# Another order of all steps in a two-layer diffusion backbone

## The chip, the cores and the metric

The kernel runs on one core of one Trainium2 chip. The metric is the device time of one execution in microseconds (us); lower is better. The engines named below are TensorE (PE, matmuls), VectorE (DVE), ScalarE (ACT), GpSimd (POOL) and SyncE (SP), whose queue issues most transfers (DMAs).

## What is computed

The reference is a backbone of two layers over 512 latent tokens and 256 context tokens of width 1024. Layer 0 mixes the tokens by windowed grouped-query attention with a sink per head, layer 1 by a gated MLP over chunks of 128 tokens. Each mixer is followed by a SwiGLU feed-forward network (FFN) with 2816 hidden channels. Before and after each part stands an RMS norm with shift, scale and gate from a modulation vector ("Ada" in the kernel). Cut to what matters here:

```python
def rmsnorm(x, g):
    xf = x.astype(jnp.float32)
    y = xf * lax.rsqrt(jnp.mean(xf * xf, axis=-1, keepdims=True) + RMS_EPS)
    return (y * g.astype(jnp.float32)).astype(x.dtype)

def modulate(h, shift, scale):
    return h * (1 + scale) + shift

def chunk_gmlp(h, w_in, b_in, ln_g, ln_b, w_s, b_s, w_o):
    bsz, n, _ = h.shape
    z = jax.nn.gelu(h @ w_in + b_in, approximate=False)
    u, v = jnp.split(z, 2, axis=-1)
    v = layernorm(v, ln_g, ln_b).reshape(bsz, n // CHUNK, CHUNK, B_GROUPS, B_GROUP_W)
    mixed = jnp.einsum('gpq,bnqgc->bnpgc', w_s, v) + b_s.T[None, None, :, :, None]
    return (u * mixed.reshape(bsz, n, B_WIDTH)) @ w_o

def swiglu(h, w_in, w_out):
    gate, up = jnp.split(h @ w_in, 2, axis=-1)
    return (jax.nn.silu(gate) * up) @ w_out
```

## The kernel before

Matrix products are done in parts: each float32 operand is split into a rounded high part (`high`, a cast on ACT, L412) and a low part (`low`, a subtraction on DVE, L419), and a product is three matmuls, high by high, low by high and high by low. Weights come from HBM as units of 128 x 2048 (1 MB, `w_raw`, two buffers) by `Stream.fetch` on SP's queue (L489); the split parts `w_hi` and `w_lo` have four buffers each.

The FFN's first half (class `FFN`, L1466) works through hidden units of 128 channels for gate and up. From unit 0 of layer 1, and over most of layer 0, it uses seven products per unit in place of eight (`product`, L1626, its matmuls at L1635), on sums of weight quarters (`diff`, L1587, on DVE, on POOL for the first units) and sums of the tokens. The results of a unit's products are gathered by `keep` (ACT, L1642), `up2`, `up1`, `gate1` (DVE, L1646 to L1654), `silu` (ACT) and `gates` (DVE). In the names, `f0product_21_6` is layer 0, unit 21, product 6.

The second half multiplies by `w_out`. Two unit pairs at its ends are plain products (`plain7`, matmuls at L1846); between them stands `seven` (L1853): the seven products of a Strassen scheme over a 2 x 2 division, each in four parts p, `product7(i, p)` (L1819). Quarters 11, 21, 22 and 12 of the weights come in halves by `fetch7` (L1746, SP). Quarter 12 is loaded twice. One copy goes into two buffers of its own, from which DVE makes the sums of 12 and 11 (`t7`, L1801). The other goes into the buffer `t7` (eight blocks of 1024 columns; quarter 21 has the second four), where POOL adds quarters 22, 11 and 21 to it in place by transfers that accumulate (`t7_add`, L1807, 256 KB each). Half 0 of quarter 22 uses the `w_raw` buffer that half 1 of quarter 12 had, and `t7_3` is the last to read that. `w7_high` and `w7_low` split a block, `a7_high` and `a7_low` the tokens; `save7` (ACT) and `add7` (DVE) hold partial results.

The end of a part is a `Chain` per block t of 128 tokens: `square_y` (ACT, L439), `rstd_y` (DVE L448 and POOL L449), `gain_y` (DVE, L1319), `add_x` (DVE, L1323), `store` (SP). Block 3 of the last layer is done in two halves of 512 columns.

At the start `warm` (L686) keeps PE at work on zeros, `turn_in` (L692) transposes the input, `rope_turn` (L909) the table of the rotary embedding, and `ada0_rows` (L709) makes the first modulation rows from weights `ada`, which load in pieces `ada0_fetch`.

The order of all this is a table. The program is written as steps; `at(time, step, ...)` gives a step a name (`key`) and its rank in the list `ORDER` (L41), and `run_plan()` issues the steps sorted by rank:

```python
        plan.append((rank.get(key, len(rank) + time), len(plan), key, step, args))

    def run_plan():
        for _, _, key, step, args in sorted(plan, key=lambda e: e[:2]):
            step(*args)
```

The order of the list is kept on each engine, and each engine and each issuing queue works in that order. A step that waits holds up all later steps of its engine; a load on SP that waits for its buffer holds up all later loads. Which buffer of a ring a step gets follows from the order as well.

Of the kernel before, what the change touches and what calls it, by code (L numbers as in the profile page):

```python
# [46 lines left out]
ada0_fetch_1 dma#2 ada0_fetch_2 ada0_fetch_4 square_in_2 turn_in_0_0 ada0_rows_out_0 turn_in_0_1 rstd_in_2 norm_in_2_0
norm_in_2_1 ada0_cols_0 turn_in_2_0 whigh_0_0 ada0_rows_1 rope_turned_0 turn_in_2_1 turned_in_0_0 ada0_rows_out_1
turn_in_3_0 <lambda> ada0_done_0 modulate0_ctx_0 ada0_cols_1 wlow_0_0 modulated_ctx_0 kv_0_4 kv_0_5 turned_in_2_0
ada0_done_1 turned_in_3_0 modulate0_0 modulated_high_0 modulated_low_0 wfetch_0_1 modulated_high_1 ada0_rows_2  # L50
ada0_rows_out_2 kv_0_2 turned_in_2_1 modulate0_ctx_1 modulate0_1 modulated_ctx_1 ada0_cols_2 kv_0_1 whigh_0_1 kv_0_0
modulated_low_1 kv_1_4 kv_1_1 kv_1_2 kv_1_5 ada0_done_2 ada0_fetch_3 rope_turned_1 modulate0_ctx_2 turned_in_0_1
modulate0_2 m2start wlow_0_1 modulated_high_2 ada0_rows_4 modulated_ctx_2 ada0_rows_3 ada0_rows_out_4 ada0_cols_4
ada0_done_4 kv_1_0 ada0_rows_out_3 ada0_cols_3 wfetch_1 whigh_1_0 wlow_1_0 whigh_1_1 kv_2_4 modulated_low_2 kv_0_3
ada0_fetch_5 kv_1_3 kv_2_3 kv_2_1 ada0_done_3 modulate0_3 modulated_high_3 modulate0_ctx_3 ada0_rows_5 modulated_ctx_3
kv_3_4 kv_2_5 kv_3_5 modulate0_ctx_4 modulated_ctx_4 modulated_high_4 kv_2_2 kv_4_5 kv_2_0 modulated_low_3
ada0_rows_out_5 ada0_cols_5 kv_3_2 kv_3_3 m2fetch_0 m2add_0 kv_3_0 kv_3_1 dma#3 ada0_fetch_6 ada0_rows_6 m2add_1
modulate0_4 <lambda>#2 ada0_done_5 modulated_high_5 modulate0_ctx_5 ada0_fetch_7 ada0_rows_7 modulated_low_4 kv_4_2
wfetch_2 kv_4_3 ada0_rows_out_6 ada0_cols_6 wlow_1_1 modulate0_5 modulated_low_5 whigh_2_0 wlow_2_0 ada0_done_6
modulate0_6 kv_4_4 ada0_rows_out_7 kv_4_0 m2fetch_1 m2add_2 m2add_3 modulated_high_6 modulated_low_6 kv_5_0 q_first_0_0  # L60
kv_5_3 whigh_2_1 ada0_cols_7 dma#4 modulated_ctx_5 ada0_done_7 modulated_high_7 wlow_2_1 modulate0_ctx_6 kv_4_1 kv_5_1
q_first_0_1 q_first_0_2 q_first_0_3 q_first_0_4 q_first_0_5 kv_5_2 kv_6_3 kv_5_5 modulate0_7 modulated_ctx_6 q_first_0_6
kv_6_0 kv_5_4 m2fetch_2 modulated_low_7 modulate0_ctx_7 kv_7_3 kv_6_1 m2add_4 kv_6_4 m2add_5 m2fetch_3 kv_6_2 kv_7_2
wfetch_3 kv_6_5 kv_7_0 q_first_0_7 kv_7_1 modulated_ctx_7 m2add_6 m2add_7 kv_7_5 kv_7_4 q_first_1_0 table_Exp k_copy_2_0
k_copy_2_1 q_rows_0 v_copy_0 k_copy_0_0 k_rope_2 k_add_2 k_copy_0_1 v_copy_1 k_copy_4_0 k_copy_4_1 v_copy_2 k_rope_0
v_copy_3 q_first_1_1 q_first_1_2 q_first_1_3 q_first_1_4 q_first_1_5 q_first_1_6 q_first_1_7 k_turn_2_1 k_add_0 v_copy_4
# [2167 lines left out]
```

## Time and profile before

| | us |
|---|---|
| median of 3 runs | 1097.65 (1097.63 to 1099.7) |
| the profiled execution | 1098.59 |
| its span | 1096.8 |
| PE busy | 1077.8 (98%), 6894 instructions |
| DVE busy | 939.1 (86%) |
| ACT busy | 601.0 (55%) |
| POOL busy | 263.1 (24%) |
| DMA traffic | 181.25 MB, mean 165 GB/s |

The parts of the span: start to 23 us, attention to 300, hidden units of layer 0 to 488, its second half to 570 or so, the gating layer to 780, hidden units of layer 1 to 970, the rest its second half. Busy time of an engine says little by itself; the windows below set the busy time of each engine in a stretch against the length of the stretch, and the timeline says of single instructions how long the engine had been idle and what ended that.

### The profile page before, as it was taken

How to read it: one execution, taken by the hardware profiler on the slowest of the kernel's cores; microseconds unless marked ns; L12 is line 12 of the kernel's file. 1: busy time of each engine (PE TensorE's matmuls, PEld its weight loads, DVE VectorE, ACT ScalarE, POOL GpSimd, SP SyncE). 2: the span in 40 equal slices, each digit the busy share in tenths (PEclk: the TensorE clock that was granted, in tenths of full speed). 3: DMA queues.
4: the chain of work that ended last, by engine and by line, in shares of the span. 5: the costliest groups of instructions: out<-in, count | busy, mean ns of one | idle time of the engine just before them, and what ended most of it. 6: DMA issues, size and time to landing. Idle time of an engine off the chain costs nothing.

```text
span 1096.8 us, 17794 instructions
## 1 busy us (share of the span) xinstructions
PE 1077.8 (98%) x6894; PEld 948.3 (86%) x6894; DVE 939.1 (86%) x1382; ACT 601.0 (55%) x1055; POOL 263.1 (24%) x268
## 2 busy tenths in 40 slices
...
GB/s 357 285 153 169 179 109 46 78 188 177 77 174 192 212 117 196 170 213 248 238 88 78 203 271 236 192 197 73 96 134 120 113 154 143 113 229 315 172 28 77
DMA packets 50392, 181.25 MB, mean 165 GB/s; under 512 B 5370, under 2 KB 9722, under 8 KB 39172
## 3 DMA queue, kind: packets, MB, share of 16 engines
...
q8 instruction: 54, 0.88, 0.3%
...
## 4 chain that ended last, share of the span: by engine, by line
PE 89%; DVE 5%; DMA 3%; issue 1%; ACT 1%; SPq 0%; DVEq 0%; POOLq 0%; POOL 0%; ACTq 0%
PE f L1635 36%; PE y L1819 12%; PE y L479 7%; PE y L1846 6%; PE v L479 4%; PE s_ps L1099 2%; PE pT_ps L1132 2%; PE o_ps L1148 2%; PE q_ps L861 1%; DMA t<-in_w 1%; PE fa L471 1%; PE fa L473 1%; PE fa L472 1%; PE u L2054 1%; PE u L2053 1%; PE u L2052 1%
## 5 line engine op out<-in xcount | busy, mean ns | idle before, releaser
L1635 PE MATMUL f<-H,w_hi 128*128 128x256 f32 x960 | 177.8, 284 | 0.5 <-DVE fc L1646 0.5
L1635 PEld LDWEIGHTS f<-H,w_hi 128*128 128x128 f32 x960 | 150.0, 192 | 1.3 <-DVE fc L1646 1.0
L1635 PE MATMUL f<-H,w_lo 128*128 128x256 f32 x480 | 135.8, 283 | 0.0
L1819 PE MATMUL y<-w_hi,s 128*128 128x512 f32 x448 | 120.6, 390 | 2.5 <-ACT s L412 1.3
L1635 PE MATMUL f<-S,w_hi 128*128 128x256 f32 x640 | 118.5, 284 | 0.5 <-ACT fc L1642 0.5
L412 ACT CAST w_hi<-T 128x1024 fp32r<-128x1024 f32 x80 | 83.7, 1047 | 58.7 <-PE f L1635 41.5
L412 ACT CAST w_hi<-w_raw 128x1024 fp32r<-128x1024 f32 x90 | 94.0, 1054 | 31.1 <-PE f L1635 11.3
L1819 PEld LDWEIGHTS y<-w_hi,s 128*128 128x128 f32 x448 | 83.9, 188 | 20.8 <-DVE s L419 1.8
L419 DVE TENSOR_TENSOR w_lo<-w_raw,w_hi 128x1024 fp32r<-128x1024 f32 (+1 forms) x81 | 96.1, 1192 | 6.4 <-ACT w_hi L412 6.1
L1635 PEld LDWEIGHTS f<-S,w_hi 128*128 128x128 f32 x640 | 99.8, 192 | 0.9 <-ACT fc L1642 0.7
L419 DVE TENSOR_TENSOR w_lo<-T,w_hi 128x1024 fp32r<-128x1024 f32 x80 | 97.3, 1219 | 2.6 <-ACT w_hi L412 2.6
L1635 PEld LDWEIGHTS f<-H,w_lo 128*128 128x128 f32 x480 | 92.1, 192 | 0.0
L1635 PE MATMUL f<-S,w_lo 128*128 128x256 f32 x320 | 90.6, 283 | 0.0
L1642 ACT COPY fc<-f 128x256 f32<-128x256 f32 x120 | 43.6, 372 | 84.2 <-PE f L1635 75.6
L1807 POOL DMA_DIRECT2D t<-in_w x48 | 42.5, 955 | 178.3 <-DMA t<-in_w 105.1
L581 DVE SCALAR_TENSOR_TENSOR acc<-ada_k,sc,acc 128x1024 f32<-128x1024 f32 x56 | 71.6, 1278 | 6.1 <-DMA ada_k<-in_ada 5.7
L595 POOL DMA_DIRECT2D acc<-acc x8 | 6.9, 868 | 286.2 <-DVE acc L581 279.1
L1819 PE MATMUL y<-w_lo,s 128*128 128x512 f32 x224 | 69.3, 391 | 1.1 <-DVE w_lo L419 1.1
L1126 POOL TENSOR_SCALAR p<-p,st 128x512 f32<-128x512 f32 (+1 forms) x64 | 59.8, 948 | 27.5 <-DVE st L1122 14.5
L1635 PE MATMUL f<-H,x 128*128 128x256 f32 x480 | 64.1, 283 | 0.0
L1110 ACT ACTIVATE p<-s_ps,st 128x512 f32<-128x512 f32 (+1 forms) x64 | 47.3, 741 | 25.9 <-DVE st L1105 22.3
L1635 PEld LDWEIGHTS f<-S,w_lo 128*128 128x128 f32 x320 | 61.4, 192 | 0.0
...
## 6 DMA issues: line engine op xcount, KB each, us to landing
w_raw<-in_w SPq DMA_DIRECT2D x67, 1024.0 KB, 5.4
ada_k<-in_ada SPq DMA_DIRECT2D x56, 512.0 KB, 5.9
ada_raw<-in_ada SPq DMA_DIRECT2D x12, 1024.0 KB, 5.4
w<-in_w SPq DMA_DIRECT2D x12, 1024.0 KB, 7.6
...
ada<-in_ada SPq DMA_DIRECT2D x8, 1024.0 KB, 8.4
t<-in_w SPq DMA_DIRECT2D x8, 1024.0 KB, 10.7
w_raw<-in_w SPq DMA_DIRECT2D x10, 512.0 KB, 7.3
```

What stands on the lines that cost most here:

```text
L412: nc.scalar.copy(out=hi, in_=src)
L419: (eng or nc.vector).tensor_tensor(out=v(lo), in0=v(src), in1=v(hi).bitcast(F32), op=ALU.subtract)
L479: nc.tensor.matmul(dst, l, w[:, n * 512:(n + 1) * 512], start=first and i == 0, stop=last and i == 2)
L581: nc.vector.scalar_tensor_tensor(out=self.acc, in0=self.raws.pop(k), scalar=sc[:, k:k + 1], in1=self.acc, op0=ALU.mult, op1=ALU.add)
L1099: nc.tensor.matmul(dst, q, keys, start=i == 0, stop=i == 1)
L1110: nc.scalar.activation(out=p[:, 0:self.n], in_=self.s[j], func=AF.Exp, scale=-1.0, bias=self.st[:, 4 + j:5 + j], accum_out=self.st[:, 8 + ...
L1126: nc.gpsimd.tensor_scalar(out=p, in0=p, scalar1=self.st[:, 12 + j:13 + j], scalar2=1.0, op0=ALU.mult, op1=ALU.mult)
L1635: nc.tensor.matmul(dst, l[:, w], r[:, k, :], start=first and k == 0 and j == 0, stop=k == 3 and j == 2, skip_group_check=True)
L1642: nc.scalar.copy(out=self.c[n][:, i * 256:(i + 1) * 256], in_=self.ps[n, 1 if i == 1 else 0])
L1807: nc.gpsimd.dma_start(out=self.tt[:, p * D + 512 * i:p * D + 512 * (i + 1)], in_=a["w"][F2[self.layer] + 1 + 2 * p + i][:, c:c + 512], acc ...
L1819: nc.tensor.matmul(self.bank7(i, j), st[:, c:c + P], w[:, z * 512:(z + 1) * 512], start=i == 1 and p == 0 and l == 0 and z == 0, stop=p == ...
L1846: nc.tensor.matmul(self.y[t][n], st[:, x + t * P:x + (t + 1) * P], parts[h][w][:, n * 512:(n + 1) * 512], start=v == 0 and h == 0 and i == ...
```

## The change

Only the table `ORDER` is another one. It has the same 3317 names, so each step and each instruction is there as often as before, and all buffers have the sizes and counts they had. A name stands 14.9 places from where it stood in the mean; the largest moves are 338 places up and 473 down. The file has two lines more, so that L1819 before is L1821 after. A few lines of the diff:

```diff
--- before.py
+++ after.py
@@ -39,359 +39,361 @@
 
 
 ORDER = """
...
-f0product_21_1 f0set_split_0 f0gate1_20 whigh_32_0 f0silu_18_1 f0fetch7_12_0_big f0keep_21_0 f0s7_S3_0 f0gates_18
-f0product_21_6 f0gates_19 f0silu_20_0 f0silu_20_1 m1halve_0 m1halve_512 m1total_0_slot wlow_32_0 whigh_32_1
-f0product_21_2 f0gate1_21 wlow_32_1 m1done_0 f0keep_21_2 f0product_21_7 f0keep_21_1 f0product_21_3 f0fetch7_11_0_raw
...
-f0product7_1_1 f0product7_1_2 f0a7_high_7_0 f0w7_high_7_1 f0a7_low_2_0 f0t7_3 f0w7_low_7_0 f0a7_low_7_0 f0s7_S2_0
...
-f0w7_high_7_3 f0a7_high_7_3 f0w7_high_7_2 f0w7_low_7_2 f0a7_high_7_2 f0w7_high_2_3 f0a7_low_7_2 f0s7_S2_2 f0a7_low_7_3
-f0w7_high_2_2 f0a7_high_2_2 f0w7_low_7_3 f0t7_add_0_11 f0s7_S2_3 f0t7_1 f0a7_low_2_2 f0product7_7_0 f0product7_7_1
...
+f0product_20_7 f0part_high_21_1 m1add_chunk_6 f0diff_21_4 f0part_high_21_3 f0product_21_1 f0up2_20 f0product_20_3
...
+whigh_32_0 f0gates_18 f0part_high_21_2 f0product_21_6 f0silu_20_0 f0part_low_21_2 f0keep_21_2 whigh_32_1 m1fetch_chunk_7
+m1fetch_gain wlow_32_0 f0silu_20_1 f0gates_19 wlow_32_1 f0product_21_5 f0keep_21_1 f0product_21_7 f0product_21_2
+f0up2_21 f0take7_0 f0product_21_4 m1add_chunk_7 m1halve_512 f0up1_20 f0gates_20 m0done_512 f0fetch7_12_0_big
...
+f0product7_1_1 f0t7_add_0_22 f0t7_0 f0w7_low_2_0 f0product7_1_2 f0a7_low_1_3 f0w7_high_7_0 f0s7_S3_2 f0t7_3
...
+f0product7_7_1 f0t7_add_0_11 f0w7_high_7_2 f0a7_high_2_2 f0w7_high_7_3 f0w7_low_7_2 f0s7_S2_1 f0w7_high_2_2 f0a7_low_7_2
+f0s7_S2_2 f0product7_7_2 f0a7_high_2_3 f0a7_low_2_2 f0w7_high_2_3 f0w7_low_7_3 f0product7_7_3 f0w7_low_2_2 f0a7_high_3_0
...
```

The pieces below show three places of it, in the order of issue on one engine.

ACT in `seven` of layer 0. `w7_5664`, `t7_5724` and the like are loaded quarters; an `s7` cast is of tokens, `act4_3425`, `act4_3971`, `act4_4430`, `act4_5055` being parts p = 0 to 3. Before:

```order
L412 CAST w_hi_5909<-t7_5724 128x1024
L412 CAST s7_5912<-act4_5055 128x512
L412 CAST w_hi_5914<-t7_5724 128x1024
L412 CAST s7_5918<-act4_4430 128x512
L412 CAST w_hi_5920<-t7_5724 128x1024
L412 CAST w_hi_5926<-t7_5724 128x1024
L412 CAST s7_5929<-act4_4430 128x512
L412 CAST s7_5986<-act4_3971 128x512
```

and in the change, where the parts are `act4_3494`, `act4_4037`, `act4_4447`, `act4_4976`:

```order
L414 CAST w_hi_5948<-t7_5694 128x1024
L414 CAST s7_5951<-act4_4447 128x512
L414 CAST w_hi_5953<-t7_5694 128x1024
L414 CAST w_hi_5958<-t7_5694 128x1024
L414 CAST s7_5975<-act4_4976 128x512
L414 CAST w_hi_5978<-t7_5694 128x1024
```

Before, `w_hi_5909` and `w_hi_5914` are blocks (7,3) and (7,2), then come `w_hi_5920`, block (2,3), and `w_hi_5926`, block (2,2). In the change `w_hi_5948` is (7,2), `w_hi_5953` is (7,3), and then comes `w_hi_5958`, block (2,2), ahead of `w_hi_5978`, block (2,3).

DVE in the hidden units of layer 1, from the last reader of unit 6's weights on. Unit 8's weights use the same buffer and load when it is free. Before, with unit 6 in `w_raw_8171` and unit 8 in `w_raw_8525`:

```order
L419 TENSOR_TENSOR w_lo_8441<-w_raw_8171,w_hi_8440 128x1024
L1650 TENSOR_TENSOR fc_8384<-f1_8371,fc_8384 128x256
L581 SCALAR_TENSOR_TENSOR acc_8443<-ada_k_7951,sc_69,acc_8443 128x1024
L1595 TENSOR_TENSOR T_8490<-w_raw_8401 128x512
L1646 TENSOR_TENSOR fc_8384<-f0_8324,fc_8384 128x256
L419 TENSOR_TENSOR w_lo_8473<-T_8366,w_hi_8472 128x1024
L1595 TENSOR_TENSOR T_8490<-w_raw_8401 128x512
L419 TENSOR_TENSOR x0_8510<-w_raw_8401,x0_8510 128x512
L1595 TENSOR_TENSOR T_8490<-T_8490,w_raw_8401 128x512
L1665 TENSOR_TENSOR act4_8362<-fc_8384,silu_8529 128x2x256
L1595 TENSOR_TENSOR T_8490<-w_raw_8401,T_8490 128x512
L419 TENSOR_TENSOR w_lo_8545<-T_8490,w_hi_8544 128x1024
```

and in the change, with unit 6 in `w_raw_7906` and unit 8 in `w_raw_8466`:

```order
L421 TENSOR_TENSOR w_lo_8449<-w_raw_7906,w_hi_8448 128x1024
L1667 TENSOR_TENSOR act4_8361<-fc_8110,silu_8484 128x2x256
L1648 TENSOR_TENSOR fc_8408<-f0_8329,fc_8408 128x256
L1597 TENSOR_TENSOR T_8534<-w_raw_7979 128x512 x2
L421 TENSOR_TENSOR x0_8503<-w_raw_7979,x0_8503 128x512
L1597 TENSOR_TENSOR T_8534<-T_8534,w_raw_7979 128x512
L583 SCALAR_TENSOR_TENSOR acc_7639<-ada_k_8464,sc_69,acc_7639 128x1024
L421 TENSOR_TENSOR w_lo_8520<-w_raw_7979,w_hi_8519 128x1024
L421 TENSOR_TENSOR w_lo_8552<-T_8363,w_hi_8551 128x1024
L421 TENSOR_TENSOR w_lo_8573<-T_8534,w_hi_8572 128x1024
L421 TENSOR_TENSOR x0_8592<-w_raw_8466,x0_8592 128x512
```

Before, DVE's first row on `w_raw_8525` is the fourth after this piece, 15 rows behind the last one on `w_raw_8171`. In the change the first row on `w_raw_8466` is the last one shown, 10 rows behind.

DVE at the end of the program. `y10`, `y11`, `y30`, `y31`, `y00`, `y01` are the accumulators of blocks 1, 3 and 0. Before:

```order
L1319 TENSOR_TENSOR tmp_11276<-y10_10527,row_10197 128x512
L448 TENSOR_SCALAR ry_11278<-msy_11269,msy_11272 128x1
L1319 TENSOR_TENSOR tmp_11276<-y11_10528,row_10197 128x512
L1323 SCALAR_TENSOR_TENSOR x_2630<-tmp_11276,ry_11278,x_2630 128x1024
L448 TENSOR_SCALAR ry_11299<-msy_11253,msy_11296 128x1
L1319 TENSOR_TENSOR tmp_11251<-y31_10469,row_10197 128x512
L1323 SCALAR_TENSOR_TENSOR x_2630<-tmp_11251,ry_11299,x_2630 128x512 x2
```

and in the change:

```order
L1325 SCALAR_TENSOR_TENSOR x_2630<-tmp_11264,ry_11270,x_2630 128x512
L1321 TENSOR_TENSOR tmp_11221<-y21_10489,row_9551 128x512
L1325 SCALAR_TENSOR_TENSOR x_2630<-tmp_11264,ry_11270,x_2630 128x512
L1325 SCALAR_TENSOR_TENSOR x_2630<-tmp_11221,ry_11261,x_2630 128x1024
L1321 TENSOR_TENSOR tmp_11296<-y00_10469,row_9551 128x512
L450 TENSOR_SCALAR ry_11301<-msy_11293,msy_11298 128x1
L1321 TENSOR_TENSOR tmp_11296<-y01_10470,row_9551 128x512
L1325 SCALAR_TENSOR_TENSOR x_2630<-tmp_11296,ry_11301,x_2630 128x1024
```

Before, block 3's second half (`y31`) comes last and its sum is written in two pieces; in the change block 3 is done earlier, and block 0 comes last, whole, with both halves of its accumulators.

## Rows read from the trace of the kernel before

**Rows 1.** The page: busy time of each engine, share of the span, instructions.

```profile
PE 1077.8 (98%) x6894; PEld 948.3 (86%) x6894; DVE 939.1 (86%) x1382; ACT 601.0 (55%) x1055; POOL 263.1 (24%) x268
```

**Rows 2.** Windows: length, then busy us (instructions) by engine, granted clock, DMA share, GB/s.

```profile
60.00:180.00 120.00, 117.47 (x727) 95.33 (x726) 109.16 (x214) 84.88 (x190) 78.03 (x84) 1.00 0.42 129
300.00:480.00 180.00, 180.00 (x1496) 179.66 (x1496) 175.07 (x241) 92.52 (x161) 3.17 (x4) 1.00 0.53 175
480.00:510.00 30.00, 28.98 (x174) 25.27 (x174) 25.50 (x36) 16.57 (x29) 4.39 (x5) 1.00 0.89 281
510.00:570.00 60.00, 56.39 (x246) 45.62 (x245) 48.72 (x59) 35.51 (x48) 16.88 (x20) 1.00 0.81 179
810.00:840.00 30.00, 29.47 (x245) 29.48 (x246) 28.17 (x41) 15.32 (x27) 0.00 (x0) 1.00 0.39 138
840.00:960.00 120.00, 120.00 (x1002) 120.00 (x1001) 105.57 (x150) 62.59 (x107) 0.35 (x1) 1.00 0.38 133
```

**Rows 3.** Chain of waits from 500 to 560 us: start, us, what.

```profile
515.72 1.23 DVE t L1801
517.38 14.76 DMA t<-in_w
```

**Rows 4.** Timeline of ACT: start, us, engine, line, what [idle before <-releaser].

```profile
532.24 1.99 ACT L412 CAST w_hi<-t 128x1024 fp32r<-128x1024 f32 x2 [8.02 <-DMA t<-in_w]
```

**Rows 5.** Timeline of PE in the product seven of layer 0.

```profile
534.81 0.73 PE L1819 MATMUL y<-w_hi,s 128*128 128x512 f32 x2 [1.32 <-ACT s L412]
```

**Rows 6.** DMA queues from 515 to 533 us: packets, MB, share of 16 engines.

```profile
q0 software_dynamic: 851, 1.55, 50.4%
```

**Rows 7.** DMA issues: transfer, queue, count, KB each, median us to landing.

```profile
w_raw<-in_w SPq DMA_DIRECT2D x67, 1024.0 KB, 5.4
t<-in_w SPq DMA_DIRECT2D x8, 1024.0 KB, 10.7
out<-x SPq DMA_DIRECT2D x3, 512.0 KB, 2.6
```

**Rows 8.** Timeline of PE, end of layer 0's hidden units.

```profile
485.78 0.50 PE L1635 MATMUL f<-S,w_hi 128*128 128x256 f32 x2 [0.52 <-ACT fc L1642]
```

**Rows 9.** Timeline of PE, layer 1's hidden units.

```profile
810.53 0.50 PE L1635 MATMUL f<-H,w_hi 128*128 128x256 f32 x2 [0.53 <-DVE fc L1646]
```

**Rows 10.** Layer 1, unit 9: SP and PE timelines; then SP's loads, 830 to 960 us.

```profile
826.80 0.33 SPq L409 DMA_DIRECT2D w_raw<-in_w  x1
848.06 1.12 PE L1635 MATMUL f<-H,x 128*128 128x256 f32 x8
DMA to landing us min/median/max: 5.1/5.3/6.1
```

**Rows 11.** Layer 0, unit 9: timelines of SP, ACT, DVE and PE.

```profile
343.83 0.33 SPq L409 DMA_DIRECT2D w_raw<-in_w  x1
350.87 0.63 ACT L412 CAST x<-w_raw 128x512 fp32r<-128x512 f32 x1 [1.74 <-DVE act L1665]
353.35 0.68 DVE L419 TENSOR_TENSOR x<-w_raw,x 128x512 fp32r<-128x512 f32 x1
354.32 0.88 PE L1635 MATMUL f<-H,x 128*128 128x256 f32 x6
```

**Rows 12.** Timeline of PE at the start.

```profile
1.79 6.57 PE L684 MATMUL warm<-idle 128*128 128x512 f32 x10 [1.79 <-DVE idle L681]
20.69 1.07 PE L718 MATMUL rows<-ada,s 128*32 128x256 f32 x16 [0.28 <-DMA ada<-in_ada]
22.76 0.47 PE L471 MATMUL kv<-w_hi,hc 128*128 128x512 f32 x1
```

**Rows 13.** Timeline of all engines at the end.

```profile
1089.94 0.39 PE L1846 MATMUL y<-w_hi,st 128*128 128x512 f32 x1
1090.42 0.60 ACT L439 ACTIVATE junk<-y 128x512 bf16<-128x512 f32 x1 [1.54 <-PE y L1846]
1092.02 1.41 DVE L1323 SCALAR_TENSOR_TENSOR x<-tmp,ry,x 128x512 f32<-128x512 f32 x2
```

More of the change, by code (lines that the diff above doesn't have):

```diff
@@ L47 @@
[L47 to L66, printed above, removed]
@@ new lines @@
+c1turned_hi_0 c3merge c2rstd_x c3square_y c3gain_y c3rstd_y f0part_high_2_0 c1turned_lo_0 f0first_half_1#2
+f0part_low_2_0 c3add_x c3gain_x c2shift_x_1 f0head_0_2 c1turned_hi_1 f0head_1_0 c1turned_lo_1 c3square_x c2turn_1
+c3rstd_x f0part_high_3_0 c2shift_x_0 c2turned_hi_1 m5start c3shift_x_0 f0head_1_1 f0diff_2_1 f0first_half_0
+f0part_high_2_2 m5fetch_chunk_1_spare m0fetch_gain c2turn_0 c3shift_x_1 c2turned_hi_0 c2turned_lo_0 f0diff_2_3
+f0diff_2_2 f0part_low_3_0 f0sum_a_S3 f0product_2_1 c2turned_lo_1 c3turn_1 f0part_low_2_2 f0sum_a_S2 f0first_half_0#2
@@ new lines @@
+f0keep_12_2 f0product_13_1 f0up2_11 f0keep_12_1 f0part_high_13_1 f0part_high_13_2 m0fetch_chunk_3_spare f0gate1_11
+f0silu_11_0 f0keep_13_0 f0product_12_3 f0product_11_4 f0silu_11_1 f0gate1_12 m0add_chunk_2 f0part_low_13_1
+f0part_low_13_2 f0gates_11 m5stack f0part_high_14_0 f0part_high_14_2 f0product_13_5 f0diff_14_1 f0part_low_14_0
+wfetch_25 f0product_12_7 f0up2_12 m1fetch_chunk_0_spare f0part_high_13_3 f0diff_14_3 f0diff_14_2 f0part_low_13_3
+f0product_13_6 f0keep_13_1 f0product_13_2 f0product_12_4 f0keep_13_2 f0product_13_7 f0up1_12 m5total_0_slot
@@ new lines @@
+f0part_high_15_3 table_Silu f0part_low_15_2 f0product_15_2 f0keep_15_0 m0fetch_chunk_6_spare f0product_15_5 f0keep_15_1
+f0diff_16_1 f0up1_14 f0diff_16_3 f0up2_14 f0silu_13_0 f0gates_12 f0product_15_6 wfetch_27 f0diff_16_2
+m0fetch_chunk_5_spare f0product_14_4 f0gate1_14 f0part_high_16_0 m0add_chunk_4 f0part_low_16_0 f0product_16_1
+f0keep_15_2 wfetch_28 f0part_high_16_2 f0part_low_16_2 wfetch_29 f0silu_13_1 m1fetch_chunk_4 f0part_low_15_3
+f0product_15_3 f0product_15_7 f0product_16_2 f0gates_13 f0part_high_16_1 f0part_low_16_1 f0product_16_5 f0silu_14_0
@@ new lines @@
+whigh_48_1 m4fetch_chunk_1 wlow_47_1 u_part_0_1 v_part_3_(3,) v1rstd v0mean wlow_48_1 wlow_48_0 m4fetch_chunk_2
+m4add_chunk_1 m4add_chunk_2 table_Gelu v0var v0rstd v0gain v1gain m4fetch_chunk_5 v0bias v3add v1bias wfetch_49
+whigh_49_0 u_part_1_0 m4fetch_chunk_4 m2mirror#2 m4add_chunk_3 v3gelu v3mean v2add v3var whigh_49_1 wfetch_50
+m4add_chunk_4 wlow_49_0 m4add_chunk_5 v2gelu v2mean v2var m4fetch_chunk_7 u_part_1_1 m4fetch_chunk_6 wlow_49_1
+u_part_2_0 whigh_50_0 whigh_50_1 wlow_50_1 m3fetch_chunk_0 ws_in wfetch_51 m3start#2 bias_in m2stack#2 v2rstd
```

655 lines of the change are left out of this document (328 added, 327 removed).

## Prediction

> **What bounds the kernel now.** I read the page's busy shares first, then the windows of the span that lose time on TensorE (PE), then the chain of waits through the worst of them, then the two ends. PE is busy 1077.8 us of a span of 1096.8, VectorE (DVE) 939.1 [rows 1]. So only what stops PE, and the two ends where PE has nothing to do, can move the time; the matmuls are the same. From 300 to 480 us PE is busy 180.00 of 180.00 at a granted clock of 1.00, the 2.4 GHz level: nothing to win there, only to lose. The windows with losses are 60 to 180 (2.53 us), 480 to 510 (1.02), 510 to 570 (3.61) and 810 to 840 (0.53) [rows 2]. With the refill of PE's pipeline after each stop and the waits of the start it is about 14 us in all; 6.5 us more lie behind the last matmul.
>
> The profiled execution took 1098.59 us, 1.8 more than its span, and stands 0.94 above the median of the runs, 1097.65. I take differences from the trace and apply them to the median. A measurement of this kernel can tell about 0.2% from no change, 2.2 us: faster means under 1095.45, slower over 1099.85.
>
> **The worst place: the product called seven in layer 0.** The chain runs through one transfer [rows 3]: the sum t7_3 on DVE (L1801) ends at 516.95; only then can SP issue the load of quarter 22, half 0, and behind it in SP's queue, at 517.38, the 1 MB load of quarter 21, half 1, which lands 14.76 us later. ACT had stood idle 8.02 us for it and casts two weight blocks in 1.99 us [rows 4]; PE stops three times, the first for 1.32 us [rows 5], 3.61 in all [rows 2], 4.1 from start to start against a pitch of 0.226 us. Meanwhile the accumulating transfers of POOL (L1807), queue q0, take 50.4% of the DMA engines [rows 6]; a 1 MB load takes 5.4 us in the kernel's median, 10.7 among these transfers [rows 7].
>
> The first pieces of order show what changes here. The casts of blocks (2,2) and (2,3) change places, so the block that PE needs first is cast first, 1.0 us off the first stop. Products (7,0) to (7,3) stay ahead of (2,2), so the PE work that covers the load is the same. The load still stands behind t7_3. That sum has moved up among DVE's rows, past three rows on 128 x 512 elements, 0.68 us each as the one of that size in [rows 11], and the accumulating transfers can begin up to 1.4 us earlier, since product 21_4, the last reader of the buffer that they fill, now precedes 21_3 (12 matmuls). But t7_3 still stands behind split blocks that wait for buffers of PE, so I bound its gain by 0 and 3 us. At 0 the first stop falls to about 0.5 and the second to 1.2: 2.4 us won. From 2 us on all 4.1 are won. I take **-3.3**. Quarter 22, half 1, is now loaded 13.6 us of PE work ahead of its product instead of 32.7; with 10.7 as its price it is still in time.
>
> **End of layer 0's hidden units.** Before, product 21_6 stands right behind 21_1 and waits 0.52 us for the copy of its result [rows 8], 0.68 from start to start. Right behind it one column sum of the modulation (L612) waits for its halves, which ACT and DVE have only just made; the rest of the 1.02 us of that window is this [rows 2], 0.94 from start to start. In the changed order two products (20_3 and 20_4) stand between 21_1 and 21_6, one, of 12 matmuls or 1.43 us, between the halves and the first of the two sums, and two plain products before the second: more than the 0.52 and the 0.94 that they have to cover, so **-1.6** (0 to -1.6). Next to be late is the plain product 0_2, which needs an accumulator that a sum of the modulation frees; the row of 0.52 is my bound, and I count nothing.
>
> **Layer 1's hidden units.** At 810.53 PE idles 0.53 us for DVE's up2 [rows 9], before product 4_4; three products instead of one now stand between 4_7 and 4_4: **-0.7**, with the refill. Against it, 2_6 now stands right behind 2_1, the pattern of [rows 8]: **+0.7**.
>
> **Weights that come later.** Two raw buffers hold the units' weights, so SP's load of unit n waits until DVE's last reader of unit n-2. Before, in layer 1, the load of unit 9 is issued at 826.80 and product 9_1 starts at 848.06 [rows 10], 21.3 us, and so from unit 9 to 21. In the changed order the last reader stands only 7.1 us of PE work (60 matmuls) ahead of the product at units 7 and 8 of layer 1 and 20 of layer 0, 8.8 at unit 4 of layer 0, 10.0 at unit 10 of layer 0 and 21 of layer 1. The second pieces of order show unit 8. What must fit is the load, 5.4 [rows 7], a cast of 0.63 and a subtraction of 0.68 [rows 11]: 6.7 us if nothing queues; 7.1 is then just enough. Unit 9 of layer 0 shows the other end: issued at 343.83, subtracted at 354.03, PE starts at 354.32 [rows 11]; 10.2 us, since cast and subtraction stand in rows that ACT and DVE work off in order. So a unit costs 0 to 3.1 us, the three 0 to 9.3; a stop lets DVE catch up, and layer 1's DVE has room (105.57 busy of 120 [rows 2]), so I take 0.5 each, **+1.5**. The Trainium skill, page "DMA: Bandwidth & Descriptors", section "Bandwidth", measures 6.15 us for 1 MB; by it the sum of the three would be 7.5 us, an estimate, and the three units would pay 0.4 each with nothing queued, which speaks against this change. The trace disagrees: 5.1 to 6.1, median 5.3, between 830 and 960 [rows 10]; the measurement decides.
>
> Unit 49, in the gating layer, has its lead cut from 24.7 to 10.9 us of PE work; load 5.4, cast 1.0 [rows 4], subtraction 1.2 (as long as t7_3 [rows 3]) need 7.6: 0 to 2, taken **+0.5**.
>
> **Start.** Ten warm-up matmuls run from 1.79 for 6.57 us; rows_1 starts at 20.69 when its load lands, and the first projection at 22.76, after transposes [rows 12]. Now the projection follows rows_1 directly; rows_1 takes 1.07, so up to 1.0 us is won. But the turn of the rope table stands ahead of the warm-ups and waits for its load, so warm-ups and transposes end some 4 us later, and transposes may still run when rows_1 could start: up to 1.0 lost. As many bytes as before are ahead of rows_1's load. **-0.5**.
>
> **Tail.** Last comes now all of token block 0 instead of half of block 3 (third pieces of order). After the last matmul, 1089.94 + 0.39, come a square of 0.60 us, the root, the gain, the sum in two halves, 1.41 together, a store of 256 KB for each, and the end at 1096.8 [rows 1, 13]. Now two squares end together and the second waits for the first, +0.5, less what the matmul before last gives, 0.1. The store is one of 512 KB, 2.6 us to landing [rows 7]; against half the bytes that is 0 to 1.3 more, I take the middle, +0.7. **+1.1** (0 to 2).
>
> **Attention, 60 to 300 us.** The same DVE work in another order. DVE is busy 109.16 of 120 us in 60 to 180, so a shift can stop PE there; to be won are the 2.53 us [rows 2]. I found no stop that goes or comes for certain: 0, bounds -2 and +2.
>
> **Sum:** -3.3 - 1.6 - 0.7 + 0.7 + 1.5 + 0.5 - 0.5 + 1.1 = -2.3; 1097.65 - 2.3 = **1095.3**.
>
> **Rivals.** (a) Late weights decide, and it gets slower. The units of 7.1 us lead pay the long chain of [rows 11], 10.2 - 7.1 = 3.1 each, 9.3 instead of 1.5: 1095.3 + 7.8 = 1103.1; at two thirds of it 1100. It decides from 2 us for each of the three on. For it: layer 0's DVE is busy 175.07 of 180 [rows 2]. Against it: layer 1's loads have 21.3 us now without a stop, so its rows have slack. Chance 0.22. (b) The gains are eaten: t7_3 comes no earlier (0.9 less won), the late units cost 3 (1.5 more) and the start wins nothing (0.5): 1095.3 + 2.9 = 1098.2. Chance 0.27, of it 0.04 over the slower bound and 0.02 under the faster one. (c) Everything fits: no late unit (-1.5), no unit 49 (-0.5), no stop behind 2_1 (-0.7), the whole 4.1 (-0.8): 1091.8. Chance 0.17. (d) The forecast, 1093.5 to 1096.5: 0.34, of it 0.27 faster.
>
> **How the numbers follow.** Faster 0.27 + 0.17 + 0.02 = 0.46; slower 0.22 + 0.04 = 0.26; the same 0.28. The range takes in (c) less its lowest part, 1090.5, by the bounds of attention, and (a) to a little over two thirds, 1102. Faster and slower are both open, so (d)'s own range stands beside it.
>
> **What would show it.** Right: ACT's idle time for the load of quarter 21 shrinks and the stops at products (2,2) and (2,3) fall under 1.7 us together; no stop at 21_6 or at the column sum; 780 to 960 loses under 2 us; 7.6 us from the last matmul to the end. Wrong: PE stops at products 7_1 and 8_1 of layer 1, with their loads issued less than 10 us before, or the window 300 to 480 is no longer full.

## The result: slower, and the profile after

| | before | after |
|---|---|---|
| median of 13 runs | 1097.83 us (1097.63 to 1099.7) | 1100.09 us (1099.51 to 1101.56) |
| ratio | | 1.0019, 95% interval 1.0011 to 1.0027 |
| the profiled execution | 1098.59 us | 1101.56 us |
| its span | 1096.8 us | 1099.8 us |

1095.3 us was forecast, so the time moved 2.3 us the other way. Each profiled execution stands above its median, by 0.8 us before and by 1.5 after, so the traces differ by 3.0 us where the medians differ by 2.3. First the windows of the changed kernel (length, then busy us of PE, PEld, DVE, ACT and POOL, granted clock, DMA share, GB/s). From the second on they answer to the lines of [rows 2]; the first answers to the line below them, of the kernel before.

```profile
60.00:90.00 30.00, 23.95 (x108) 19.80 (x107) 24.89 (x35) 13.95 (x28) 5.69 (x5) 0.89 0.43 135
60.00:180.00 120.00, 112.40 (x671) 91.16 (x670) 105.44 (x196) 78.43 (x173) 69.53 (x77) 0.97 0.44 133
300.00:480.00 180.00, 180.00 (x1491) 179.41 (x1491) 174.22 (x239) 92.38 (x162) 2.65 (x3) 1.00 0.49 162
480.00:510.00 30.00, 30.00 (x213) 28.02 (x212) 29.18 (x39) 17.81 (x31) 2.24 (x3) 1.00 0.93 331
510.00:570.00 60.00, 59.96 (x265) 49.29 (x264) 52.14 (x65) 37.27 (x50) 19.07 (x22) 1.00 0.90 198
810.00:840.00 30.00, 30.00 (x253) 30.00 (x252) 27.52 (x39) 16.00 (x30) 0.00 (x0) 1.00 0.40 141
840.00:960.00 120.00, 120.00 (x1001) 119.88 (x1000) 106.36 (x153) 60.40 (x106) 0.85 (x1) 1.00 0.40 134
```

```profile
60.00:90.00 30.00, 28.76 (x138) 23.69 (x137) 25.46 (x41) 18.46 (x37) 8.32 (x9) 1.00 0.55 174
```

The stops that the change was to remove are gone: 510 to 570 us was 56.39 busy and is 59.96, 480 to 510 and 810 to 840 are full. What is lost is lost in attention: from 60 to 180 us PE was busy 117.47 of 120 and is busy 112.40, at a granted clock of 0.97, and nearly all of the loss is in the first 30 us (28.76 busy before, 23.95 after). The longest waits of PE in the whole program say where (tile, line, what ended the wait: us in total, times, the longest):

```profile
PE q_ps L863 <- DVE klo L421: 6.1, 1, 6.1
PE rope L917 <- DMA ident<-in_ident: 4.0, 1, 4.0
PE s_ps L1101 <- ACT p L1112: 1.9, 3, 1.0
```

One wait of 6.1 us stands out. PE's timeline after, from the transposes of the keys (`kT`, `k_turn`) to the first score of attention:

```profile
74.65 2.78 PE L1021 MATMUL kT<-ident,kr 128*128 128x128 f32 x24
83.48 1.19 PE L863 MATMUL q_ps<-HA,w_hi 128*128 128x512 f32 x2 [6.05 <-DVE klo L421]
84.47 0.63 PE L863 MATMUL q_ps<-HA,w_lo 128*128 128x512 f32 x1
84.90 1.05 PE L863 MATMUL q_ps<-HA,w_hi 128*128 128x512 f32 x2
...
88.72 0.63 PE L863 MATMUL q_ps<-HA,w_hi 128*128 128x512 f32 x2
...
91.47 0.39 PE L1101 MATMUL s_ps<-khi,q_X 128*128 128x512 f32 x1
```

and the same places before:

```profile
74.74 2.78 PE L1019 MATMUL kT<-ident,kr 128*128 128x128 f32 x24
77.56 0.73 PE L861 MATMUL q_ps<-HA,w_hi 128*128 128x512 f32 x2
...
80.41 0.61 PE L861 MATMUL q_ps<-HA,w_hi 128*128 128x512 f32 x2
...
84.49 0.47 PE L1099 MATMUL s_ps<-khi,q_X 128*128 128x512 f32 x1 [1.19 <-DVE klo L419]
```

Before, the query projection `q_step_2_0` followed the transposes at once. After, it starts 5.92 us later, and its first twelve matmuls take 5.24 us (83.48 to 88.72) instead of 2.85 (77.56 to 80.41): one matmul to the next takes 0.43 us (84.47 to 84.90), where it took 0.23. That is 2.4 us more. The stop of 1.35 us from start to start that the first score had before (1.19 idle) is gone, so it starts 6.99 us later.

Why DVE ends the wait: the six `k_turn` steps write six PSUM banks of one pool; for each, `k_split` casts the bank on ACT (`khi`) and takes the rest on DVE (`klo`). `q_step_2_0` is the first step on a pool that is opened after that one is closed, and what it waits for, by the rows below and the runs a_turn to b_dose, is the split of the transpose that PE issues first. DVE's timeline after, and below it before:

```profile
77.16 1.27 DVE L421 TENSOR_TENSOR klo<-kT,khi 128x512 fp32r<-128x512 f32 x2
...
82.06 1.28 DVE L421 TENSOR_TENSOR klo<-kT,khi 128x512 fp32r<-128x512 f32 x2
83.26 0.68 DVE L961 TENSOR_TENSOR q_rot<-q_rot 128x512 f32<-128x512 f32 x1
83.86 1.28 DVE L421 TENSOR_TENSOR klo<-kT,khi 128x512 fp32r<-128x512 f32 x2
```

```profile
76.83 0.68 DVE L419 TENSOR_TENSOR klo<-kT,khi 128x512 fp32r<-128x512 f32 x1
77.54 1.41 DVE L419 TENSOR_TENSOR q_X<-q_rot,q_X 64x512 fp32r<-64x512 f32 x2
78.97 0.69 DVE L419 TENSOR_TENSOR klo<-kT,khi 128x512 fp32r<-128x512 f32 x1
```

Before, `k_turn_2_1` is first, and its split is DVE's first, done at 77.51. After, `k_turn_4_0` is first, DVE's splits come in the order 2_1, 4_1, 0_1, 4_0, 0_0, 2_0, and that of 4_0, the fourth, ends at 83.34; PE starts at 83.48.

Landmarks on PE, after less before, in us of the two profiled executions:

| landmark | later by | so the part before it gave |
|---|---|---|
| first projection | -0.1 | start -0.1 |
| `q_step_2_0` | +5.92 | |
| first score | +6.99 | |
| first hidden product, layer 0 | +8.28 | attention +8.4 |
| first product of seven, layer 0 | +6.64 | hidden units -1.6 |
| end of seven, layer 0 | +2.36 | seven -4.3 |
| last matmul | +1.98 | the rest -0.4 |
| end of the span | +3.0 | tail +1.0 |

### The profile page after: what moved, and what is told of

Read it like the earlier page. It is cut to its first block, busy times and chain, and to the rows that moved or that the text cites. A ratio compares the mean times of both kernels' runs of the same rounds, so it can differ in the third digit from the quotient of the medians.

```text
span 1099.8 us, 17843 instructions
## 1 busy us (share of the span) xinstructions
PE 1079.7 (98%) x6894; PEld 951.6 (87%) x6894; DVE 941.5 (86%) x1382; ACT 599.8 (55%) x1055; POOL 264.9 (24%) x268
## 4 chain that ended last, share of the span: by engine, by line
PE 92%; DVE 4%; DMA 1%; POOL 1%; issue 1%; ACT 1%; SPq 0%; DVEq 0%; ACTq 0%; POOLq 0%
PE f L1637 37%; PE y L1821 14%; PE y L481 7%; PE y L1848 6%; PE v L481 4%; PE s_ps L1101 3%; PE o_ps L1150 3%; PE pT_ps L1134 3%; PE q_ps L863 3%; PE fa L475 1%; PE fa L473 1%; PE fa L474 1%; PE u L2054 1%; PE u L2056 1%; PE u L2055 1%; POOL w_lo L421 1%
## 5 line engine op out<-in xcount | busy, mean ns | idle before, releaser
L1821 PE MATMUL y<-w_hi,s 128*128 128x512 f32 x448 | 120.2, 389 | 0.0
L421 DVE TENSOR_TENSOR w_lo<-T,w_hi 128x1024 fp32r<-128x1024 f32 x80 | 97.0, 1219 | 11.0 <-ACT w_hi L414 10.6
L1821 PEld LDWEIGHTS y<-w_hi,s 128*128 128x128 f32 x448 | 84.0, 188 | 17.7 <-ACT r L1829 0.3
L1821 PE MATMUL y<-w_lo,s 128*128 128x512 f32 x224 | 69.1, 390 | 0.0
L1128 POOL TENSOR_SCALAR p<-p,st 128x512 f32<-128x512 f32 (+1 forms) x64 | 55.7, 902 | 34.2 <-DVE st L1124 26.3
L1107 DVE CUSTOM_DVE_ANT_0 s_ps<-s_ps,mask,nsink 128x512 f32<-128x512 f32 (+1 forms) x64 | 51.3, 821 | 14.4 <-PE s_ps L1101 13.5
```

The costliest lines, as they stand in the source:

```text
L421: (eng or nc.vector).tensor_tensor(out=v(lo), in0=v(src), in1=v(hi).bitcast(F32), op=ALU.subtract)
L1107: nc.vector.tensor_tensor_reduce(out=s, in0=s, in1=self.msk, scale=-1.0, scalar=nsink[:, h:h + 1], op0=ALU.add, op1=ALU.min, accum_out=sel ...
L1128: nc.gpsimd.tensor_scalar(out=p, in0=p, scalar1=self.st[:, 12 + j:13 + j], scalar2=1.0, op0=ALU.mult, op1=ALU.mult)
L1821: nc.tensor.matmul(self.bank7(i, j), st[:, c:c + P], w[:, z * 512:(z + 1) * 512], start=i == 1 and p == 0 and l == 0 and z == 0, stop=p == ...
```

## The experiments

Names with a_ are edits of the changed kernel, names with b_ of the kernel before. Each ratio is to the kernel before on the same chip; the medians come from several chips, so across runs the ratios are compared.

| run | us | ratio, 95% interval |
|---|---|---|
| a_turn | 1093.71 | 0.9955, 0.9943 to 0.9968 |
| a_split | 1093.86 | 0.9953, 0.994 to 0.9967 |
| b_turn | 1102.6 | 1.0038, 1.0025 to 1.0051 |
| a_turn_tail | 1092.86 | 0.9947, 0.9935 to 0.9959 |
| b_seven | 1095.11 | 0.9972, 0.9961 to 0.9983 |
| b_cast | 1096.75 | 0.9991, 0.9981 to 1.0 |
| b_units | 1097.45 | 0.9994, 0.9985 to 1.0003 |
| a_best1 | 1092.36 | 0.995, 0.9937 to 0.9962 |
| b_dose | 1100.14 | 1.0021, 1.0012 to 1.003 |
| a_late | 1101.52 | 1.0034, 1.0022 to 1.0046 |
| a_best2 | 1092.98 | 0.9954, 0.9941 to 0.9966 |

### a_turn and a_split: first transpose and its split put together

a_turn exchanges two transposes on PE, a_split two splits on ACT and DVE; nothing else moves.

```diff
 a_turn
-k_copy_4_1 k_rope_0 whigh_3_0 k_add_0 k_turn_4_0 wlow_3_0_512_1024 whigh_3_1 ...
-wlow_3_0_0_512 q_add_0 q_rows_1 k_turn_2_1 k_turn_4_1 k_split_2_1 k_split_4_1 ...
+k_copy_4_1 k_rope_0 whigh_3_0 k_add_0 k_turn_2_1 wlow_3_0_512_1024 whigh_3_1 ...
+wlow_3_0_0_512 q_add_0 q_rows_1 k_turn_4_0 k_turn_4_1 k_split_2_1 k_split_4_1 ...
 a_split
-... k_turn_2_1 k_turn_4_1 k_split_2_1 k_split_4_1 ... k_split_4_0 q_add_1
+... k_turn_2_1 k_turn_4_1 k_split_4_0 k_split_4_1 ... k_split_2_1 q_add_1
```

> The changed order with two names exchanged: k_turn_2_1 is again the first of the six transposes of keys, k_turn_4_0 the second. Theory: the first of the six takes the PSUM bank that q_step_2_0 uses next, so q_step_2_0 waits for that transpose's split; with k_turn_2_1 first it waits for k_split_2_1, the first split on DVE, and not for k_split_4_0, the fifth. PE's idle 6.05 us before q_step_2_0 goes, and with it the stretch of half clock behind it, together 8.7 us; score_0_0 then waits about 1.4 us for k_split_0_0 as in the kernel before. Expected 1100.1 - 8.7 + 1.4 = 1092.8 us (1092.0 to 1093.6), granted clock 1.00 in 60 to 90 us. Rival: DVE is late with all splits in the changed order, whichever transpose comes first; then the stop only moves to score_0_0 and the time stays at 1098 to 1100.

> The changed order with k_split_4_0 and k_split_2_1 exchanged: k_turn_4_0 is still the first transpose, but its split is now the first on ACT and DVE too. Theory: only the match of first transpose and first split counts, so the same gain as when the transposes are exchanged: 1092.8 us (1092.0 to 1093.6), no idle time of PE over 1 us before q_step_2_0. Rival (the lateness of DVE as a whole): 1098 to 1100. Second rival (k_turn_4_0 is itself late, through its copies): 1094 to 1098, PE waiting for k_turn_4_0's operand.

(`k_split_4_0` is the fourth split on DVE, not the fifth.) In a_turn `q_step_2_0` starts at 77.15, in a_split at 77.47, both at full pace (0.24 us from one matmul to the next), and both kernels are 0.45% faster than before. PE's timeline of a_turn, and below it the first row of that place in a_split:

```profile
77.15 0.72 PE L863 MATMUL q_ps<-HA,w_hi 128*128 128x512 f32 x2 [0.67 <-DVE klo L421]
...
83.90 0.50 PE L1101 MATMUL s_ps<-khi,q_X 128*128 128x512 f32 x1 [1.00 <-DVE klo L421]
```

```profile
77.47 0.73 PE L863 MATMUL q_ps<-HA,w_hi 128*128 128x512 f32 x2 [0.52 <-DVE klo L421]
```

The two names cost 7.1 us between the first projection and the first hidden product of layer 0 (262.3 us after, 255.2 in a_turn, 253.9 before), and 7.0 us by the two ratios (1.0019 to 0.9955). The spans differ by 8.0 (1099.8 to 1091.8), but 0.9 of that lies ahead of the first projection, where both kernels have the same order. It is neither transpose nor split by itself, but the distance of the two in their two orders: either exchange removes it, down to the waits of 0.67 and 0.52 us shown.

Of the 8.4 us that the landmarks put on attention, 1.3 stay in a_turn and 1.2 in a_split. Part of them is PE's waiting for ACT's `p` (L1112) behind the first score: 1.6 us in both, where the kernel before waits 1.0. No run took this rest apart.

### b_turn: the same exchange in the kernel before

```diff
-... q_first_1_6 q_first_1_7 k_turn_2_1 k_add_0 v_copy_4
-k_turn_4_1 ... q_rows_1 q_swap_1 k_turn_4_0
+... q_first_1_6 q_first_1_7 k_turn_4_0 k_add_0 v_copy_4
+k_turn_4_1 ... q_rows_1 q_swap_1 k_turn_2_1
```

> The kernel before with k_turn_2_1 and k_turn_4_0 exchanged, nothing else. Theory: the loss of the changed order appears in the kernel before: q_step_2_0 waits for k_split_4_0, which ended at 81.86 us there, so PE idles about 4.3 us; score_0_0's stop of 1.35 us is then covered, net +3.0 to +3.2: 1101.0 us. If the granted clock falls after this stop as it did in the changed order (2.5 us more): 1103.4. Rival (it is the rest of the changed order that makes DVE late): 1097.8, no change.

The stop appears in the kernel that never had it, and with it matmuls at half the pace (PE's timeline):

```profile
82.02 0.70 PE L861 MATMUL q_ps<-HA,w_hi 128*128 128x512 f32 x2 [4.62 <-DVE klo L419]
...
82.84 1.05 PE L861 MATMUL q_ps<-HA,w_hi 128*128 128x512 f32 x2
...
86.44 0.63 PE L861 MATMUL q_ps<-HA,w_hi 128*128 128x512 f32 x2
```

Twelve matmuls take 4.42 us (82.02 to 86.44) instead of 2.85. The first score is 4.70 us later, the end of the span 3.3: 1.2 us come back in the product seven of layer 0, where PE, now later, does not make the first of its three stops, the 1.32 us of [rows 5]. By the ratio the time rose by 4.2 us, between the 3.2 expected without a fall of the clock and the 5.6 with one.

### b_dose: a shorter wait

```diff
-... q_first_1_7 k_turn_2_1 k_add_0 v_copy_4
+... q_first_1_7 k_add_0 k_turn_0_1 k_turn_2_1 v_copy_4
```

(`k_turn_0_1` moves up from its old place further on.)

> The kernel before with k_turn_0_1 as the first of the six transposes instead of k_turn_2_1 (k_add_0 moved ahead of it, which DVE had done 3 us earlier). In the trace of before, DVE's split of it ended at 79.66, so q_step_2_0 starts at 79.7 instead of 77.56: an idle time of 2.2 us, between the 0.9 us after which the granted clock stayed at the 2.4 GHz level and the 4.62 us after which the matmuls ran at half pitch. Theory 1 (the bank's releaser sets the wait, as in the other runs): idle 2.2 us at q_step_2_0. What the clock does is open. If it holds, the pitch is 0.227 us at once and the loss is 2.1 us by score_0_0, less what the later stop there (1.35 before) gives back, so about +1 us at the end. If it falls, pitch 0.43 us for some matmuls, 1.5 to 2.5 us more, +2.5 to +3.5 at the end. Rival (another bank than the first transpose's): no wait at q_step_2_0.

```profile
79.72 0.70 PE L861 MATMUL q_ps<-HA,w_hi 128*128 128x512 f32 x2 [2.30 <-DVE klo L419]
80.26 0.39 PE L861 MATMUL q_ps<-HA,w_lo 128*128 128x512 f32 x1
80.49 0.62 PE L861 MATMUL q_ps<-HA,w_hi 128*128 128x512 f32 x2
```

The wait is 2.30 us, as the end of DVE's second split, that of 0_1, says, and the clock holds: 0.23 us from one matmul to the next at once. The first score starts 0.77 us later and the span is 1.1 longer, near what was expected, but on the way 0.4 us comes back in layer 0's product seven and 0.7 is added in layer 1's, where PE stops at 1045.19 for 0.52 us for DVE and does not in the profiled execution of the kernel before. The median rose by 2.3; the profiled executions stand 0.5 under it here (1099.68) and 0.7 above it before (1098.59 to 1097.87), which is the difference. The size of this loss is therefore known only as 1.1 to 2.3.

### a_turn_tail: and the old end of the program

a_turn with the order of the last 51 steps (from `f1plain7_9_1` on) as before.

```diff
+f1product7_4_2 wlow_86_1 f1product7_4_3 whigh_87_0 f1add7_p7d_0 ...
...
+c3square_y_512_1024 c3rstd_y#4 c3gain_y_512_1024 c3add_x_0_512 c3store_0_512 ...
```

> The changed order with the two transposes exchanged as in a_turn, and with the last 51 steps (from f1plain7_9_1 on) in the relative order that they have in the kernel before, so that block 3 comes last in two halves. Theory: the tail of the changed order costs the difference of the times from the last matmul to the end, 7.5 against 6.5 us, so 1.0 us less than a_turn: 1091.8 us. Rival: the store's landing and the end of the program take the same whatever comes last; then as a_turn, 1092.8.

0.85 us less in the median than a_turn (1093.71 to 1092.86), 0.5 in the span. The intervals overlap, so a gain is not shown; the sign agrees with the tail's +1.0 in the landmarks.

### b_seven and b_cast: the product seven of layer 0

b_seven gives the kernel before the changed order from `f0plain7_0_3` to `f0product7_4_3`; b_cast only casts the block that PE needs first ahead of the other.

```diff
 b_cast
-... f0w7_low_7_2 f0a7_high_7_2 f0w7_high_2_3 f0a7_low_7_2 f0s7_S2_2 f0a7_low_7_3
-f0w7_high_2_2 f0a7_high_2_2 f0w7_low_7_3 ...
+... f0w7_low_7_2 f0a7_high_7_2 f0a7_high_2_2 f0w7_high_2_2 f0a7_low_7_2 f0s7_S2_2
+f0a7_low_7_3 f0w7_high_2_3 f0w7_low_7_3 ...
```

> The kernel before, with the steps from f0plain7_0_3 to f0product7_4_3 (layer 0's product seven) in the relative order that they have in the change. Theory: the gain of the change there stands alone. The accumulating transfers of quarter 11 wait for a weight split that now stands behind block (2,1), so POOL issues none while quarter 21, half 1, loads; that load lands in 10.4 us at most instead of 14.76, and the three stops, 4.1 us from start to start, go. Expected 3.5 to 4.3 us under the kernel before. Rival: the gain comes from t7_3's earlier place (0.6 us) and the exchanged casts (1.0); then 1.6 us under.

> The kernel before, with ACT's cast of block (2,2) and of the tokens for it ahead of the cast of block (2,3); nothing else moves, and the load of quarter 21, half 1, lands as late as before. The prediction put 2.4 us on this alone (first stop to about 0.5, second to 1.2, third gone): 2.4 us under the kernel before. Rival: DVE's rows behind it still hold the third stop, since the tokens of block (2,3) come after work on other blocks: 1.0 to 1.5 us under.

The windows, b_seven above and b_cast below:

```profile
510.00:570.00 60.00, 59.96 (x265) 49.34 (x264) 52.77 (x65) 37.37 (x50) 16.83 (x19) 1.00 0.81 178
```

```profile
510.00:570.00 60.00, 58.59 (x256) 47.43 (x255) 51.04 (x62) 36.99 (x50) 17.29 (x20) 1.00 0.79 180
```

From the product's first matmul to its last, the casts alone take 2.3 us off (80.6 to 78.3) and the whole order 3.6 (to 77.0). Less arrives at the end: 1.3 and 3.2 us of span, 0.9 and 2.5 of the median (intervals 0 to 2.1 and 1.9 to 4.3), so b_cast misses its expected 2.4. Some 0.8 us of each goes in layer 1's product seven, where PE waits for DVE and does not in the profiled execution of the kernel before; b_cast's row:

```profile
1042.79 0.73 PE L1819 MATMUL y<-w_lo,s 128*128 128x512 f32 x2 [0.53 <-DVE w_lo L419]
```

Why this stop comes is open; b_dose, with the order of before in both products, has it too. What the whole order has over the casts shows in b_seven's timelines of SP, ACT and POOL, beginning with the load of quarter 21, half 1:

```profile
516.87 0.69 SPq L409 DMA_DIRECT2D t<-in_w  x1
```

```profile
527.45 1.06 ACT L412 CAST w_hi<-t 128x1024 fp32r<-128x1024 f32 x1 [0.17 <-DMA t<-in_w]
```

```profile
514.80 0.88 POOL L1807 DMA_DIRECT2D t<-in_w  x1 [1.89 <-issue]
523.70 1.81 POOL L1807 DMA_DIRECT2D t<-in_w  x2 [8.02 <-DVE s L419]
```

The load is issued 0.5 us earlier than in [rows 3], and the product's first matmul is 0.7 earlier too (505.37 to 506.04), so against PE nothing is gained by `t7_3`. But the load takes 10.6 us from issue to the cast that waits for it, not 14.9 (517.38 to 532.24). POOL starts no accumulating transfer from 515.7 to 523.7, where before it started three between 518 and 522.6; its queue q0 moved 0.52 MB during the load instead of 1.23. In b_cast, where the load takes 14.1 (517.39 to the cast at 531.45), POOL's order is the old one. Load time and POOL's transfers go together in these runs; no run changed POOL's alone. That the transfers lengthen the load is likely, but not shown.

### b_units: the end of layer 0's hidden units

```diff
-f0product_21_1 ... f0keep_21_0 f0s7_S3_0 f0gates_18
-f0product_21_6 f0gates_19 ... m1halve_0 m1halve_512 m1total_0_slot ...
-f0product_21_2 ... f0keep_21_1 f0product_21_3 ...
+f0product_21_1 ... f0keep_21_0 f0product_21_2 f0s7_S3_0
+f0gates_18 f0product_21_6 f0keep_21_1 f0product_21_3 f0gates_19 ...
+wlow_32_0 whigh_32_1 f0gate1_21 wlow_32_1 m1total_0_slot ...
```

> The kernel before, with product 21_2 between 21_1 and 21_6, and with product 21_3 between 21_6 and the column sum m1total_0. Theory: each of the three stops in 485 to 489 us is covered by a product of 1.43 us: 1.6 us under the kernel before. Rival: the products that were moved up make later ones wait for their own copies and splits, and half of it comes back: 0.8 us under.

The three stops go, but with products 21_2 and 21_3 used up a new one of 1.45 us stands at 21_4, which waits for DVE:

```profile
PE f L1635 <- DVE fc L1646: 1.8, 2, 1.3
```

(1.3 idle here, 0.5 that of [rows 9].) So my way of filling the gap wins nothing clear of the noise, 0.9994, where 1.6 us were expected; the changed order, which fills it with products of unit 20, keeps its 1.6.

### a_late: one unit's load later

DVE's last read of unit 6's weights moves behind the rows up to unit 7's first split, so that layer 1's unit 8 loads later.

```diff
-... f1part_low_6_1 f1product_6_5 f1part_low_6_2 f1part_high_7_0
+... f1part_low_6_1 f1product_6_5 f1part_high_7_0
-... f1diff_7_1 f1diff_7_3 f1part_low_7_0 f1product_7_1
+... f1diff_7_1 f1diff_7_3 f1part_low_7_0 f1part_low_6_2 f1product_7_1
```

> The changed kernel with the last reader of unit 6's raw weights (DVE's split of its block 2) moved behind four DVE rows, so that the load of layer 1's unit 8 is issued about 2.8 us later, at 823.6 instead of 820.86 in the time of the changed kernel's trace. Theory (the late weights only just fit, so the mechanism that was feared is real and only its size was off): landing at 829.0, ACT's cast 0.63, DVE's subtraction 0.68, product 8_1 at 830.4 instead of 829.88: a stop of 0.5 to 1.5 us there, none before, and the same at the end of the span. Rival (the lead has slack that the trace does not show): no stop at product 8_1, the end where it was.

The load of unit 8 on SP and product 8_1 on PE in the changed kernel:

```profile
820.86 0.33 SPq L411 DMA_DIRECT2D w_raw<-in_w  x1
```

```profile
829.88 1.60 PE L1637 MATMUL f<-H,x 128*128 128x256 f32 x12
```

PE's timeline of a_late at product 8_1 (this execution runs 2.19 us ahead of the changed kernel's up to here):

```profile
828.51 0.50 PE L1637 MATMUL f<-H,x 128*128 128x256 f32 x2 [0.32 <-ACT x L414]
829.24 1.46 PE L1637 MATMUL f<-H,x 128*128 128x256 f32 x10 [0.22 <-DVE x L421]
```

Against PE's own time the load is issued 4.0 us later, more than I meant (822.67, with the 2.19 in it, to 820.86), and PE loses 1.57 us around product 8_1. The ratio is 0.15% above the changed kernel's, but the two intervals overlap, so the loss rests on the trace. So the price feared for late weights is real, but this unit had some 2.4 us to spare.

### a_best1 and a_best2: toward the best order

a_best1 is a_turn_tail with transposes and splits in one order, 2_1, 4_0, 0_0, 4_1, 0_1, 2_0; a_best2 also exchanges two splits:

```diff
 a_best2
-... k_split_0_0 v_copy_5 q_sin_1 k_split_4_1 q_add_1
-k_split_0_1 k_turn_2_0 ...
+... k_split_0_0 v_copy_5 q_sin_1 k_split_0_1 q_add_1
+k_split_4_1 k_turn_2_0 ...
```

> The changed order with k_turn_2_1 first, the tail of the kernel before (both as in a_turn_tail), and the splits of keys in the order 2_1, 4_0, 0_0, 4_1, 0_1, 2_0, their transposes likewise. Theory: score_0_0 needs the splits 0_0 and 4_0, which DVE now ends two places earlier, so its stop of 0.9 us goes: 0.9 us under a_turn_tail, which was 5.5 us under the kernel before, so 6.4 us under it. Rival: q_add_1 and the weight splits on DVE shift by as much and score_0_0 waits all the same: 5.5 us under.

> As a_best1, with the splits of k_turn_0_1 and k_turn_4_1 exchanged, so that DVE splits 0_0 and 0_1 one after the other, 0.6 us earlier for 0_1. Theory: score_0_0 waits for the split of 0_1 alone, its stop of 1.04 us falls to about 0.4, and the end comes 0.6 earlier: 1091.8 us, 0.9945 of before. Rival (score_0_0 needs 4_1 as well, or the query's halves): the stop stays at 1.0 and the time at 1092.4.

In a_best1 the wait before `q_step_2_0` is gone, but the first score still stops for 0.88 us, since it waits for split 0_1 (in a_best2, where that split comes earlier, this stop goes), which I had taken to be early enough. In a_best2 another comes instead (PE's timeline):

```profile
85.19 0.73 PE L863 MATMUL q_ps<-HA,w_hi 128*128 128x512 f32 x2 [1.32 <-ACT q_rot L943]
```

On ACT the copy of the query that PE waits for runs at 84.54, behind a cast (83.26) that has waited 3.11 us for DVE's `q_add_1`, which is behind the splits. Both expectations missed by their gain. a_turn_tail, a_best1 and a_best2 cannot be told apart by their intervals; each beats both kernels, by some 0.5%.

## Why the prediction was wrong

**The step that failed is the attention term**: "The same DVE work in another order ... I found no stop that goes or comes for certain: 0, bounds -2 and +2." It measured +8.4: 7.1 of it is the new wait with the slow matmuls behind it, which a_turn takes away, and 1.3, inside the bounds, is the rest. The stop stood in the two orders: PE's first transpose and DVE's first split belonged together before and not after. I compared the order on each engine with its older self, where the split of 4_0 had moved only from third to fourth, and not PE's order with DVE's, where the pair that hands over the bank had come apart. The bounds were taken from the stops that could go (2.53 us in [rows 2]) and mirrored; a new wait is not bounded by old ones. a_turn, a_split and b_turn show this term both ways. The measured 1100.09 lies inside the stated 1090.5 to 1102, but the upper part of that range was drawn for late weights: that it holds the result is luck.

Term by term against the landmarks:

- **Seven, layer 0: -3.3, measured -4.3.** The casts were right inside the product: 2.4 by the working, 2.3 in b_cast, where the first stop falls to 0.55 us, the second to 0.86 and the third goes. The rest came, but not by the reason given: `t7_3` gains only 0.6 us against PE in the changed kernel and nothing in b_seven, not the 2 that the working wanted for all 4.1. The load itself was shorter. b_seven has 3.6 of the 4.3; the other 0.7 was not taken apart.
- **End of the units: -1.6, measured -1.6.** The mechanism held in the changed kernel, and b_units shows that it depends on which products fill the gap.
- **Layer 1: -0.7 at 4_4 right; +0.7 at 2_6 wrong.** I read 2_6 as right behind 2_1. On PE, 2_1 starts at 773.49 and 2_6 at 783.51, with five steps between; there is no stop.
- **Late weights: +1.5, measured 0.** Windows 300 to 480 and 810 to 840, where the three units are, are full. The lead of 7.1 us was counted at the place where DVE's row stands in the order; DVE worked ahead of its place, and unit 8's load was issued 9.0 us before its product, not 7.1. a_late puts the limit at some 2.4 us less than that, near the 6.7 us that load, cast and subtraction need with nothing queued. The 6.15 us that the prediction took from the Trainium skill, page "DMA: Bandwidth & Descriptors", section "Bandwidth", were measured on transfers issued from GpSimd; these loads are SP's, so their median of 5.3 [rows 10] does not contradict the page.
- **Unit 49: +0.5, measured 0.** Its weights were split at 673.08, 1.4 us before the product.
- **Start: -0.5, measured -0.1.** The turn of the rope table waits 3.97 us for its load and transposes hold `rows_1` up to 21.66, as feared. Between executions this stretch moves by up to 1.1 us (the first projection at 22.66 here, at 21.57 in a_late, with the same order), so -0.1 cannot be told from -0.5.
- **Tail: +1.1, measured +1.0.** From the last matmul to the end 7.5 us, where 6.5 were; 7.6 was named.

Without attention the terms measured come to -5.4 us, nearest to rival (c), everything fits. With a_turn they arrive, less the 1.3 that stay in attention: its trace is 4.0 us under that of before from the first projection on, and 0.9955 of 1097.65 is 1092.7. Rival (a) had the sign of the result, but its mechanism did not act: no unit was late. All that the prediction named as proof of being right came true, and the kernel was slower: those signs watched the places of the change that I had already priced, none the place priced at 0.
